# A hybrid recurrent decoder layer: scans behind the first level's multiplications, and a reordered beginning

## Chip, cores and metric

The kernel runs on one core of a Trainium2 chip. The metric is the device time of one execution in microseconds, the median over repeated runs; lower is better.

## The reference

One step of one decoder layer, for a new sequence of 512 tokens and for 8 sequences that go on by one token each (520 columns in all), in float32. A recurrent layer with two branches, then an MLP with squared ReLU; both are scaled and shifted by a modulation that is computed from a conditioning vector. Cut to what is computed:

```python
cs = silu(c)
sh1, sc1, g1, sh2, sc2, g2 = split(cs @ w_mod + b_mod, 6)
h = rmsnorm(x, norm1_g) * (1 + sc1) + sh1
qa, fa, ia, oga, xb, yb, ga, gb = split(h @ w_in, 8)      # 1024 columns each
# branch A: HGRN2, 8 heads: S_t = diag(f_t) S_(t-1) + k_t outer v_t, o_t = S_t^T q_t
o, S_new = hgrn2(silu(qa), k, ia, logf, st_hg)
o_a = rmsnorm(o, hg_onorm_g) * silu(oga)
# branch B: causal conv of width 4, two gates, linear recurrence
xc, buf = causal_conv(xb, st_conv, lru_conv_w, lru_conv_b)
r  = sigmoid(blockdiag(xc, lru_wa) + lru_ba)
ig = sigmoid(blockdiag(xc, lru_wx) + lru_bx)
hseq, h_last = rglru(xc, r, ig, lru_lambda, st_lru)       # h_t = a_t h_(t-1) + sqrt(1 - a_t^2) (i_t x_t)
o_b = hseq * gelu(yb)
merged = sigmoid(ga) * (o_a @ w_branch_a) + sigmoid(gb) * (o_b @ w_branch_b)
x = x + g1 * (merged @ w_out)
h2 = rmsnorm(x, norm2_g) * (1 + sc2) + sh2
x = x + g2 * (square(relu(h2 @ w_ff1)) @ w_ff2)
y = rmsnorm(x, final_norm_g)
```

The outputs are y for both groups of tokens, and the new states of both branches.

## The kernel before

Activations lie transposed: 128 features on the partitions and 520 tokens along a row, 8 such blocks for the width of 1024. Float32 products are made of three reduced-precision ones: weight and activation are each split into a high and a low half, and TensorE (PE) multiplies high by high, high by low and low by high. A tile of weights (1024 x 128) comes by DMA as `wst`; ScalarE (ACT) casts the high half (`whi`, L112), VectorE (DVE) subtracts to get the low one (`wlo`, L115); in the beginning the same two are called `fhi` and `flo`. A product is 128 x 260, half of the 520 columns.

**The order.** Most of the kernel is put in order by the scheduler of the tile framework, from priorities and its own costs; each engine then works its list through, in that order. `behind(ins, first)` (L171) adds an order without a semaphore: `ins` may not be placed ahead of `first`. The beginning, `begin` (from L1575 on), is different: there `self.nc` is a wrapper (`InOrder`, L50) that chains PE, ACT and DVE each in the order in which the code is written.

**The beginning.** Four row blocks of x come in and PE transposes them by a product with the identity into eight PSUM banks, which `whole` copies to SBUF as `xT` (tiles `ma`). Their squares give the norm; `spread_root` spreads the root over the partitions with PE (`pb<-rsd`). `px` is one PSUM tile into which several small transposes go: `rm` (modulation's bias and norms; copied out as `pm`), `xsn` (samples; copied out as `xsr`), and `rb`, `ra`, `rc`, `rd` (parameters of the recurrences, copied out as `pl` and `pa`). The modulation for h comes in four pieces of 256 features: `piece` multiplies the conditioning by 1 MB of `w_mod` (`pt<-wm,cT`) and has ACT copy it out (`modev`), `piece_cols` turns it on PE (`pt<-pick,modev`), `piece_mod` adds and scales on DVE (`modT`). `rooted(k)` multiplies a block of x by the root (`xn<-ma,pb`), `scaled` makes h of it: high half on ACT, low on DVE, and the 8 samples' part on GpSimd (POOL, `fs`). So a piece gives two blocks of h, and `products(n, k, k+1)` adds their 12 products to the n-th of three output tiles (n = 0, 1, 2: the f, q and gate columns of the first head) before the next piece goes on. The three tiles' PSUM slots are `self.first`: two of the pool `mm`, in whose two slots x was transposed (banks 0 and 1 in one, 2 and 3 in the other), and two of `ps`.

**Heads and recurrent branch.** The heads are taken in pairs. `heads_prompt` computes the attention-like matrix within chunks of 128 by levels b = 1, 2, 4, ... 64: at each level PE multiplies pieces of X (L655 for b = 1, L660 for 2 to 32, L664 for 64), then DVE multiplies halves of X by factors in place (L676 for b = 1, L672 after), and PE's next level reads them. PE goes on with the products of the next weight tiles (L151) between two levels. Beside that, `rg_x`, `rg_scans` and `rg_y` work on the recurrent branch in pairs of blocks too: ACT makes exponentials, a square and a root (L825 to L832), DVE multiplies gates (`gate<-gate,xc`, L838), scans (L840), and keeps the last column (L841 to L844); `rg_y` makes the gate y of its output (L853 to L858).

Of the kernel before, what the change touches and what calls it, by code (L numbers as in the profile page):

```python
# [6 lines left out]
F32 = mybir.dt.float32  # L7
# [69 lines left out]
class Kernel:  # L77
# [548 lines left out]
    def heads_prompt(self, hs):  # L626
# [17 lines left out]
        while b < C:  # L644
# [23 lines left out]
            with self.together():  # L668
                for x in range(2):
                    half = halves(x, b, n)  # L670
                    if b > 1:
                        last = nc.vector.tensor_tensor(half, half, factors(tbs, x, b), OP.mult)  # L672
                    else:
                        for e, f in enumerate(fs):
                            t2 = f[:, :L].rearrange("p (n two) -> p n two", two=2)
                            nc.vector.tensor_tensor(half[:, e, :, 0], half[:, e, :, 0], t2[:, :, x], OP.mult)  # L676
            if b == 2:
                self.head_sample_state(hs[1], last)
            if b == 1:
# [138 lines left out]
    def rg_scans(self, ns):  # L818

        nc = self.nc  # L820
        aa = []
        for n in ns:
            r = self.rg[n][0]
            a = self.slot(self.rgp, "ag")
            self.grouped(nc.scalar.activation(a, r, AF.Exp, scale=self.c8n[:, n:n + 1]))  # L825
            self.grouped(nc.scalar.activation(r, r, AF.Tanh, scale=self.c8[:, n:n + 1]))
            u = self.slot(self.rgp, "xc")
            last = nc.scalar.activation(u, a, AF.Square)
            nc.vector.scalar_tensor_tensor(u, u, 1.0, r, OP.add, OP.mult)
            aa.append((a, u))  # L830
        for n, (a, u) in zip(ns, aa):
            root = nc.scalar.activation(u, u, AF.Sqrt)  # L832
            self.behind(root, last)
            last = root
        self.group, self.sigmoids = last, []
        for n, (a, u) in zip(ns, aa):
            g = self.rg[n][1]
            nc.vector.tensor_tensor(g, g, u, OP.mult)  # L838
            hs = self.slot(self.rgp, "hs")
            nc.vector.tensor_tensor_scan(hs[:, :L], a[:, :L], g[:, :L], 0.0, OP.mult, OP.add)  # L840
            nc.vector.tensor_tensor(hs[:, L:], a[:, L:], self.h0[:, :, n], OP.mult)  # L841
            nc.vector.tensor_tensor(hs[:, L:], hs[:, L:], g[:, L:], OP.add)
            nc.vector.tensor_copy(self.hlast[:, n, 0:1], hs[:, L - 1:L])
            nc.vector.tensor_copy(self.hlast[:, n, 1:9], hs[:, L:])  # L844
            self.rg[n] = hs
# [780 lines left out]
    def begin(self):  # L1626
# [74 lines left out]
        self.norm_root()  # L1701
        eye = self.diagonals()
        whole(act, 5, 4, 6, 7)
        whole(dve, 0)
        split_first(0)
        px, pr = ps(), ps()
        own = px[:, 144:457]
        nc.tensor.transpose(px[:, 64:128], rm, self.ident[:64, :64])
        for k in range(KO):
            nc.tensor.transpose(px[:, k * NB:(k + 1) * NB], self.xsn[:, k * 128:(k + 1) * 128], self.ident[:NB, :NB])  # L1710
        spread = pb()
        self.spread_root(spread, pr, *eye)
        pm = self.consts.tile([128, 64], F32, name="pm")
        dve(pm, px[:, 64:128])
# [1 line left out]
        for part in (1, 4):  # L1716
            c = self.bmod[:, part * 8:part * 8 + 8]
            nc.vector.tensor_scalar(c, c, 1.0, None, OP.add)
        whole(act, 1)
        p = self.piece(0, pieces[0])  # L1720
        split_first(1)
        self.piece_cols(p)
        self.xr = self.xn.rearrange("p t d -> p (t d)").rearrange("p (k n) -> p k n", n=L)
        rooted = lambda k: nc.vector.tensor_tensor(self.xr[:, k], self.xT[k][:, :L], spread, OP.mult)

# [7 lines left out]
        rooted(0)  # L1733
        dve(xsr, px[:, :KO * NB].rearrange("p (k b) -> p k b", b=NB))
        nc.vector.tensor_tensor(xs, xsr, pr[:, None, :NB].to_broadcast([128, KO, NB]), OP.mult)
        rooted(1)
        self.piece_mod(p)
        split_rest(0)
        scaled(0, 1)
        split_first(2)  # L1740
        split_rest(1)
        whole(act, 2, 3)
        split_rest(2)

        self.first = [mm()[:, :, :HALF], mm()[:, :, :HALF], [ps()[:, :HALF], ps()[:, :HALF]]]
        acc = [[self.first[0][:, s] for s in range(2)], [self.first[1][:, s] for s in range(2)], self.first[2]]

        def products(n, *ks, only=slice(0, 3)):
# [7 lines left out]

        for i in range(3):
            ks = 2 * i, 2 * i + 1
            products(0, *ks)
            p = self.piece(i + 1, pieces[i + 1])  # L1760
            products(1, *ks, only=slice(0, 1))
            if i == 0:
                nc.tensor.transpose(px[:, 128:144], rb, self.ident[:16, :16])
                self.parameters_in(own, *par)
                pl = self.hc.tile([128, 16], F32, name="pl")
                dve(pl, px[:, 128:144])
                dve(self.pa, self.pa_ps)
            self.piece_cols(p)
            rooted(2 * i + 2)
            self.piece_mod(p)  # L1770
            rooted(2 * i + 3)
            scaled(2 * i + 2, 2 * i + 3)
            products(1, *ks, only=slice(1, 3))
            if i == 1:
                self.bounds(pl)
                self.exponentials()
                nc.scalar.activation(self.act0, self.act0, AF.Sigmoid)
            products(2, *ks)
        for k in range(KO):
            pool.tensor_copy(self.xT[k][:, L:], xsr[:, k])  # L1780
            pool.dma_start(self.xT_d[k], self.xT[k])
# [124 lines left out]
```

## Time and profile before

| | us |
|---|---|
| median of 3 runs | 1017.22 |
| lowest, highest | 1016.69, 1019.72 |
| the profiled execution | 1015.0 |
| its span in the trace | 1013.2 |
| PE busy | 992.3 (98%) |
| DVE busy | 673.8 (67%) |
| ACT busy | 512.2 (51%) |
| POOL busy | 130.4 (13%) |

The profiled execution is one of its own; times of single instructions come from it. A row of the timeline gives start, duration (us), engine, line, operation, written tile <- read tiles, shapes and count, and in brackets the idle time of the engine before it with what ended it. Neighbouring instructions of a kind stand in one row, whose duration goes from the first one's start to the last one's end. A row's start counts from the start of the span. The beginning takes until 53 us; the two stretches with the long waits of PE among the heads lie at 288 and 378 us.

### The profile page before, as it was taken

The page shows a single profiled execution, that of the slowest core. Times are in us where ns is not written, and L with a number is a line of the kernel's source. Part 1 is how long each engine was busy: PE and PEld are TensorE (multiplying, and loading weights), DVE is VectorE, ACT ScalarE, POOL GpSimd, SP SyncE. Part 2 cuts the span into 40 slices and gives each one's busy share as a digit, 9 for nine tenths or more (in the row PEclk, how much of TensorE's full clock was granted, in tenths as well). Part 3 has the DMA queues.
Part 4 walks back from the last instruction along what each step waited for, and adds up shares of the span by engine and source line. Part 5 has one row for each costly group of instructions (what it writes and reads, how often), then busy time and mean ns, then how long its engine had stood idle before and what let it go on. Part 6 is the DMA issues. An engine that isn't in the chain of part 4 may idle for free. (4 is left out here: it accounts for less than half of the span.)

```text
span 1013.2 us, 23554 instructions
## 1 busy us (share of the span) xinstructions
PE 992.3 (98%) x9738; PEld 964.7 (95%) x9738; DVE 673.8 (67%) x1417; ACT 512.2 (51%) x963; POOL 130.4 (13%) x253
## 2 busy tenths in 40 slices
PE   6999999999999999999999999999999999999997
PEld 5899999999989999999999999999999999999996
DVE  7686867695785867346233448777767776777685
ACT  6364745735654573345111224466555645646663
POOL 4320000000000010002000000022321331232050
PEclk9999999999999999999999999999999999999998
DMA  9974354344344444339756787322672483273242
GB/s 298 314 214 119 97 164 127 103 122 135 107 137 116 124 147 127 95 98 304 205 167 177 231 245 207 102 86 50 151 176 64 98 196 104 53 175 86 63 84 85
DMA packets 205373, 145.80 MB, mean 144 GB/s; under 512 B 6742, under 2 KB 193774, under 8 KB 205258
## 3 DMA queue, kind: packets, MB, share of 16 engines
q1 hardware_dynamic: 194034, 128.08, 43.1%
q0 software_dynamic: 11216, 16.18, 7.4%
q8 instruction: 76, 1.25, 0.5%
q14 instruction: 31, 0.25, 0.1%
q10 hardware_dynamic: 16, 0.03, 0.0%
HBM read 123.61 MB, written 13.39 MB: 135 GB/s over the span
## 5 line engine op out<-in xcount | busy, mean ns | idle before, releaser
L151 PE MATMUL mm<-h,whi 128*128 128x260 f32 (+1 forms) x2944 | 488.5, 285 | 0.0
L151 PEld LDWEIGHTS mm<-h,whi 128*128 128x128 f32 x2944 | 409.2, 188 | 2.9 <-issue 1.4
L151 PE MATMUL mm<-h,wlo 128*128 128x260 f32 x1472 | 302.4, 285 | 0.0
L115 DVE TENSOR_TENSOR wlo<-wst,whi 128x1024 fp32r<-128x1024 f32 x164 | 200.0, 1221 | 133.5 <-ACT whi L112 132.2
L112 ACT CAST whi<-wst 128x1024 fp32r<-128x1024 f32 x164 | 171.7, 1049 | 213.6 <-PE mm L151 166.2
L151 PEld LDWEIGHTS mm<-h,wlo 128*128 128x128 f32 x1472 | 229.5, 188 | 0.9 <-issue 0.6
L151 PE MATMUL mm<-a,whi 128*128 128x260 f32 x512 | 83.0, 284 | 0.0
L151 PEld LDWEIGHTS mm<-a,whi 128*128 128x128 f32 x512 | 70.0, 188 | 2.1 <-ACT whi L112 1.6
L885 POOL DMA_DIRECT2D t<-obT_d x8 | 4.3, 541 | 396.9 <-PE pb L790 300.1
L151 PE MATMUL mm<-a,wlo 128*128 128x260 f32 x256 | 51.4, 282 | 0.0
L1262 DVE TENSOR_TENSOR f<-f 128x260 f32<-128x260 f32 x64 | 27.3, 426 | 27.8 <-ACT f L1257 27.2
L1254 POOL TENSOR_TENSOR ft<-ft,fsh 128x8 f32<-128x8 f32 x28 | 18.4, 658 | 206.6 <-DVE ft L1248 206.6
L1251 ACT ACTIVATE ft<-ft,fsh 128x512 f32<-128x512 f32 (+2 forms) x36 | 24.0, 675 | 36.0 <-DVE ft L1248 36.0
L151 PE MATMUL mm<-b,whi 128*128 128x260 f32 x256 | 41.7, 285 | 0.0
L151 PEld LDWEIGHTS mm<-a,wlo 128*128 128x128 f32 x256 | 39.4, 188 | 0.0
L151 PEld LDWEIGHTS mm<-b,whi 128*128 128x128 f32 x256 | 35.0, 188 | 2.1 <-ACT whi L112 2.1
L672 DVE TENSOR_TENSOR X<-X,tb 128x512 f32<-128x512 f32 x48 | 30.9, 684 | 5.4 <-PE ps L660 4.2
L1296 POOL DMA_DIRECT2D ma<-snap x28 | 26.5, 960 | 40.1 <-issue 32.3
L1278 POOL DMA_DIRECT2D ma<-snap x28 | 26.4, 943 | 38.0 <-DMA ma<-snap 22.7
L1257 ACT ACTIVATE f<-ft 128x520 f32<-128x520 f32 (+1 forms) x36 | 20.8, 587 | 15.0 <-POOL ft L1255 13.0
L580 ACT ACTIVATE st<-st,fkq 128x128 f32<-128x128 f32 x64 | 19.8, 395 | 14.1 <-DMA st<-in_state_hgrn_dram 12.4
L151 PE MATMUL mm<-b,wlo 128*128 128x260 f32 x128 | 25.6, 282 | 0.0
(576 smaller groups left out, 1865.5 us busy)
## 6 DMA issues: line engine op xcount, KB each, us to landing
wst<-in_w_in_dram SPq DMA_DIRECT2D x64, 512.0 KB, 4.1
wst<-in_w_mod_dram SPq DMA_DIRECT2D x32, 512.0 KB, 3.8
wst<-in_w_ff_dram SPq DMA_DIRECT2D x64, 256.0 KB, 3.6
wst<-in_w_ff_dram SPq DMA_DIRECT2D x32, 512.0 KB, 4.7
wm<-in_w_mod_dram SPq DMA_DIRECT2D x8, 1024.0 KB, 10.8
st<-in_state_hgrn_dram SPq DMA_DIRECT2D x8, 512.0 KB, 6.7
vb<-vd SPq DMA_DIRECT2D x8, 512.0 KB, 3.7
out_dram<-st SPq DMA_DIRECT2D x8, 512.0 KB, 3.9
```

The costliest lines, as they stand in the source:

```text
L112: ins = self.nc.scalar.copy(hi, st)
L115: self.nc.vector.tensor_tensor(lo, st, hi.bitcast(F32), OP.subtract)
L151: self.last_product = self.nc.tensor.matmul(ps[s][:, :c.stop - c.start], x, y[:, c], start=first and n == 0, stop=last and n == 2)
L580: nc.scalar.activation(st[:, b], st[:, b], AF.Copy, scale=fkq[:, 0, b:b + 1])
L672: last = nc.vector.tensor_tensor(half, half, factors(tbs, x, b), OP.mult)
L885: nc.gpsimd.dma_start(t, self.obT_d[n])
L1251: nc.scalar.activation(t[:, :p], t[:, :p], AF.Relu, bias=sh[:, 0:1])
L1254: eng.tensor_tensor(t[:, p:], t[:, p:], sh[:, 1:9], OP.add)
L1257: nc.scalar.activation(f, self.two(self.ft)[:, a:a + n], AF.Square)
L1262: self.nc.vector.tensor_tensor(f[:, n], f[:, a], f[:, b], op)
L1278: nc.gpsimd.dma_start(x[1][:, b], v[:, :n], accum_op=OP.add)
L1296: nc.gpsimd.dma_start(x[t][:, a], s[p], accum_op=OP.add)
```

## The change

In `rg_scans` the two gate multiplications of a pair are kept in `self.scans`; in `heads_prompt` they are put behind the last of the level-1 multiplications of X. Each scan reads its gate, so it follows. In `begin`, nineteen transposes of the identity into PSUM tiles that are overwritten later are added at four places (9, 3, 4 and 3), the copies of banks 0 and 1 go to ACT behind the first cast, the first low half `flo` moves ahead of the first scaling, the casts for tiles 1 and 2 move behind the first h, the parameters' transposes move ahead of the first products and their copies from DVE to ACT, and in the first round tiles 0 and 1 get their products ahead of the second piece.

```diff
@@ -673,7 +673,10 @@
                     else:
                         for e, f in enumerate(fs):
                             t2 = f[:, :L].rearrange("p (n two) -> p n two", two=2)
-                            nc.vector.tensor_tensor(half[:, e, :, 0], half[:, e, :, 0], t2[:, :, x], OP.mult)
+                            last = nc.vector.tensor_tensor(half[:, e, :, 0], half[:, e, :, 0], t2[:, :, x], OP.mult)
+            if b == 1:
+                for ins in self.scans:
+                    self.behind(ins, last)
             if b == 2:
                 self.head_sample_state(hs[1], last)
             if b == 1:
@@ -828,6 +831,7 @@
             last = nc.scalar.activation(u, a, AF.Square)
             nc.vector.scalar_tensor_tensor(u, u, 1.0, r, OP.add, OP.mult)
             aa.append((a, u))
+        self.scans = []
         for n, (a, u) in zip(ns, aa):
             root = nc.scalar.activation(u, u, AF.Sqrt)
             self.behind(root, last)
@@ -835,7 +839,7 @@
         self.group, self.sigmoids = last, []
         for n, (a, u) in zip(ns, aa):
             g = self.rg[n][1]
-            nc.vector.tensor_tensor(g, g, u, OP.mult)
+            self.scans.append(nc.vector.tensor_tensor(g, g, u, OP.mult))
             hs = self.slot(self.rgp, "hs")
             nc.vector.tensor_tensor_scan(hs[:, :L], a[:, :L], g[:, :L], 0.0, OP.mult, OP.add)
             nc.vector.tensor_tensor(hs[:, L:], a[:, L:], self.h0[:, :, n], OP.mult)
@@ -1701,14 +1705,22 @@
         self.norm_root()
         eye = self.diagonals()
         whole(act, 5, 4, 6, 7)
-        whole(dve, 0)
         split_first(0)
+        whole(act, 0, 1)
+
+        def busy(out, n):
+
+            for _ in range(n):
+                nc.tensor.transpose(out[:, :128], self.ident, self.ident)
+
+        spread = pb()
+        busy(spread, 9)
         px, pr = ps(), ps()
         own = px[:, 144:457]
         nc.tensor.transpose(px[:, 64:128], rm, self.ident[:64, :64])
         for k in range(KO):
             nc.tensor.transpose(px[:, k * NB:(k + 1) * NB], self.xsn[:, k * 128:(k + 1) * 128], self.ident[:NB, :NB])
-        spread = pb()
+        busy(spread, 3)
         self.spread_root(spread, pr, *eye)
         pm = self.consts.tile([128, 64], F32, name="pm")
         dve(pm, px[:, 64:128])
@@ -1716,10 +1728,14 @@
         for part in (1, 4):
             c = self.bmod[:, part * 8:part * 8 + 8]
             nc.vector.tensor_scalar(c, c, 1.0, None, OP.add)
-        whole(act, 1)
+        split_rest(0)
         p = self.piece(0, pieces[0])
-        split_first(1)
+        self.first = [mm()[:, :, :HALF]]
+        busy(self.first[0][:, 0], 4)
         self.piece_cols(p)
+        nc.tensor.transpose(px[:, 128:144], rb, self.ident[:16, :16])
+        self.parameters_in(own, *par)
+        busy(self.first[0][:, 0], 3)
         self.xr = self.xn.rearrange("p t d -> p (t d)").rearrange("p (k n) -> p k n", n=L)
         rooted = lambda k: nc.vector.tensor_tensor(self.xr[:, k], self.xT[k][:, :L], spread, OP.mult)
 
@@ -1733,16 +1749,19 @@
         rooted(0)
         dve(xsr, px[:, :KO * NB].rearrange("p (k b) -> p k b", b=NB))
         nc.vector.tensor_tensor(xs, xsr, pr[:, None, :NB].to_broadcast([128, KO, NB]), OP.mult)
+        self.piece_mod(p)
         rooted(1)
-        self.piece_mod(p)
-        split_rest(0)
         scaled(0, 1)
+        split_first(1)
         split_first(2)
+        pl = self.hc.tile([128, 16], F32, name="pl")
+        act(pl, px[:, 128:144])
+        act(self.pa, self.pa_ps)
         split_rest(1)
         whole(act, 2, 3)
         split_rest(2)
 
-        self.first = [mm()[:, :, :HALF], mm()[:, :, :HALF], [ps()[:, :HALF], ps()[:, :HALF]]]
+        self.first += [mm()[:, :, :HALF], [ps()[:, :HALF], ps()[:, :HALF]]]
         acc = [[self.first[0][:, s] for s in range(2)], [self.first[1][:, s] for s in range(2)], self.first[2]]
 
         def products(n, *ks, only=slice(0, 3)):
@@ -1756,26 +1775,23 @@
 
         for i in range(3):
             ks = 2 * i, 2 * i + 1
-            products(0, *ks)
+            n = 1 if i else 2
+            for m in range(n):
+                products(m, *ks)
             p = self.piece(i + 1, pieces[i + 1])
-            products(1, *ks, only=slice(0, 1))
-            if i == 0:
-                nc.tensor.transpose(px[:, 128:144], rb, self.ident[:16, :16])
-                self.parameters_in(own, *par)
-                pl = self.hc.tile([128, 16], F32, name="pl")
-                dve(pl, px[:, 128:144])
-                dve(self.pa, self.pa_ps)
+            products(n, *ks, only=slice(0, 1))
             self.piece_cols(p)
             rooted(2 * i + 2)
             self.piece_mod(p)
             rooted(2 * i + 3)
             scaled(2 * i + 2, 2 * i + 3)
-            products(1, *ks, only=slice(1, 3))
+            products(n, *ks, only=slice(1, 3))
             if i == 1:
                 self.bounds(pl)
                 self.exponentials()
                 nc.scalar.activation(self.act0, self.act0, AF.Sigmoid)
-            products(2, *ks)
+            if i:
+                products(2, *ks)
         for k in range(KO):
             pool.tensor_copy(self.xT[k][:, L:], xsr[:, k])
             pool.dma_start(self.xT_d[k], self.xT[k])
```

How this moves instructions, at three places. On PE, at the beginning, from the first piece (`pt<-wm,cT`) to the second; before:

```order
L69 MATMUL pt<-wm,cT 32x256 x8
L69 MATMUL pt<-pick,modev 128x9 x2
L69 MATMUL mm<-h,fhi 128x260 x8
L69 MATMUL mm<-h,flo 128x260 x4
L69 MATMUL pt<-wm,cT 32x256 x8
L69 MATMUL mm<-h,fhi 128x260 x4
L69 MATMUL ps<-ident,ra 128x16
L69 MATMUL ps<-ident,rb 128x57
L69 MATMUL ps<-ident,rc 128x64
L69 MATMUL ps<-ident,rd 128x96 x2
L69 MATMUL pt<-pick,modev 128x9 x2
```

and now (`mm<-ident` are identity transposes):

```order
L69 MATMUL pt<-wm,cT 32x256 x8
L69 MATMUL mm<-ident 128x128 x4
L69 MATMUL pt<-pick,modev 128x9 x2
L69 MATMUL ps<-ident,ra 128x16
L69 MATMUL ps<-ident,rb 128x57
L69 MATMUL ps<-ident,rc 128x64
L69 MATMUL ps<-ident,rd 128x96 x2
L69 MATMUL mm<-ident 128x128 x3
L69 MATMUL mm<-h,fhi 128x260 x8
L69 MATMUL mm<-h,flo 128x260 x4
L69 MATMUL mm<-h,fhi 128x260 x8
L69 MATMUL mm<-h,flo 128x260 x4
L69 MATMUL pt<-wm,cT 32x256 x8
```

The transposes of `ra` to `rd` come ahead of the first product, and 24 products of tiles 0 and 1 (12 before) ahead of the second piece.

On ACT, from the first cast to the second `modev`; before:

```order
L69 CAST fhi<-wst 128x1024
L69 COPY ma<-mm 128x512
L69 COPY modev<-pt 128x256
L69 CAST fhi<-wst 128x1024
L69 ACTIVATE h<-xn,modT 128x512 x2
L69 CAST fhi<-wst 128x1024
L69 COPY ma<-mm 128x512 x2
L69 COPY modev<-pt 128x256
```

and now:

```order
L69 COPY ma<-mm 128x512 x2
L69 COPY modev<-pt 128x256
L69 ACTIVATE h<-xn,modT 128x512 x2
L69 CAST fhi<-wst 128x1024 x2
L69 COPY pl<-ps 128x16
L69 COPY pa<-ps 128x313
L69 COPY ma<-mm 128x512 x2
L69 COPY modev<-pt 128x256
```

The two `ma<-mm` copies of banks 2 and 3 now stand behind h, two casts and the two copies that were DVE's. On DVE at the same place the rows from the first scaling on were

```order
L69 TENSOR_TENSOR xn<-ma,pb 128x512
L69 COPY xsr<-ps 128x64
L69 TENSOR_TENSOR xhs<-xsr,ps 128x64
L69 TENSOR_TENSOR xn<-ma,pb 128x512
L69 TENSOR_TENSOR modT<-pt,pm 128x18
L69 TENSOR_TENSOR modT<-modT,pm 128x18
L69 TENSOR_TENSOR flo<-wst,fhi 128x1024
L69 SCALAR_TENSOR_TENSOR h<-xn,modT,h 128x512 x2
L69 TENSOR_TENSOR flo<-wst,fhi 128x1024 x2
L69 COPY pl<-ps 128x16
```

and are, from the copy of pm on:

```order
L69 COPY pm<-ps 128x64
L69 TENSOR_SCALAR pm<-pm 128x8 x2
L69 TENSOR_TENSOR flo<-wst,fhi 128x1024
L69 TENSOR_TENSOR xn<-ma,pb 128x512
L69 COPY xsr<-ps 128x64
L69 TENSOR_TENSOR xhs<-xsr,ps 128x64
L69 TENSOR_TENSOR modT<-pt,pm 128x18
L69 TENSOR_TENSOR modT<-modT,pm 128x18
L69 TENSOR_TENSOR xn<-ma,pb 128x512
L69 SCALAR_TENSOR_TENSOR h<-xn,modT,h 128x512 x2
L69 TENSOR_TENSOR flo<-wst,fhi 128x1024 x2
```

The low half `flo` is ahead of the first `xn`, and `modT` is behind one scaling in place of two.

On DVE, in the third pair of heads, from the second gate on; before:

```order
L838 TENSOR_TENSOR gate<-gate,xc 128x520
L840 SCALAR_TENSOR_TENSOR hs<-ag,gate 128x512
L842 TENSOR_TENSOR hs<-hs,gate 128x8
L841 TENSOR_TENSOR hs<-ag,pa 128x8
L840 SCALAR_TENSOR_TENSOR hs<-ag,gate 128x512
L843 COPY hlast<-hs 128x1
L115 TENSOR_TENSOR wlo<-wst,whi 128x1024
L844 COPY hlast<-hs 128x8
L842 TENSOR_TENSOR hs<-hs,gate 128x8
L843 COPY hlast<-hs 128x1
L676 TENSOR_TENSOR X_798<-X_798,ma 128x256 x2
L855 SCALAR_TENSOR_TENSOR y<-y 128x520
```

and now:

```order
L115 TENSOR_TENSOR wlo<-wst,whi 128x1024
L676 TENSOR_TENSOR X_817<-X_817,ma 128x256 x2
L859 SCALAR_TENSOR_TENSOR y<-y 128x520
L676 TENSOR_TENSOR X_817<-X_817,ma 128x256 x2
L842 TENSOR_TENSOR gate<-gate,xc 128x520 x2
L684 TENSOR_TENSOR a_4018<-ps,mdiag 128x256
L861 TENSOR_TENSOR y<-y 128x520
L844 SCALAR_TENSOR_TENSOR hs<-ag,gate 128x512
L846 TENSOR_TENSOR hs<-hs,gate 128x8
L845 TENSOR_TENSOR hs<-ag,pa 128x8
L844 SCALAR_TENSOR_TENSOR hs<-ag,gate 128x512
L688 COPY_PREDICATED a_4018<-mask_179,ps 128x256
```

Both gates and both scans went from ahead of the four `X<-X,ma` to behind them; `wlo` stayed ahead. In the first two pairs the order was this way round before, and doesn't change; in the fourth pair the four multiplications stand together, and nothing of the recurrent branch but the small `hs<-ag,pa` right ahead of them. Between the levels b = 2 and b = 4 of the third pair PE now has 46 products (31 before), and between b = 4 and b = 8 of the fourth 51 (38 before).

## The prediction

> **What bounds the kernel now.** I read the page's busy times first, then the waits of PE, then the stretches around those waits.
>
> ```profile
> span 1013.2 us, 23554 instructions
> PE 992.3 (98%) x9738; PEld 964.7 (95%) x9738; DVE 673.8 (67%) x1417; ACT 512.2 (51%) x963; POOL 130.4 (13%) x253
> ```
>
> PE is busy for 992.3 of 1013.2 us, so all that any edit here can win is the 21 us in which it stands still, and time in which it runs at a lower clock. The waits of PE (what it waited for: us in total, times, longest) tell which of these the change reaches:
>
> ```profile
> PE ps L660 <- DVE X L676: 3.3, 4, 1.0
> PE mm L69 <- ACT h L69: 2.5, 1, 2.5
> ```
>
> The first row is the level-2 products of the heads, waiting for the level-1 multiplications; the second is the first product of the beginning, waiting for h. The other waits (for inputs at the very start, one or two tenths elsewhere) are left as they are.
>
> The beginning, as PE and the clock saw it:
>
> ```profile
> 16.80 0.61 PE L69 MATMUL pt<-pick,modev 128*128 128x9 f32 x4 [0.49 <-ACT modev L69]
> 19.91 2.28 PE L69 MATMUL mm<-h,fhi 128*128 128x260 f32 x8 [2.50 <-ACT h L69]
> 23.10 1.30 PE L69 MATMUL pt<-wm,cT 128*32 128x256 f32 x16
> 25.01 0.23 PE L69 MATMUL ps<-ident,ra 16*128 16x16 f32 x1
> 25.44 0.38 PE L69 MATMUL ps<-ident,rd 96*128 96x96 f32 x2
> 27.09 1.12 PE L69 MATMUL ps<-h,fhi 128*128 128x260 f32 x8
> 28.04 0.64 PE L69 MATMUL ps<-h,flo 128*128 128x260 f32 x4
> 30.50 1.07 PE L69 MATMUL pt<-wm,cT 128*32 128x256 f32 x16
> ```
>
> At full clock eight products take 28.04 - 27.09 = 0.95 us, 0.12 each. The first twelve took from 19.91 to 23.10, about 3.2 us, and the windows (length, PE busy, granted clock, DMA share, GB/s) say why:
>
> ```profile
> 16.80:20.20 3.40, 0.90 (x6) 1.00 1.14 323
> 20.20:23.60 3.40, 3.31 (x20) 0.50 1.09 348
> ```
>
> After a stretch with 0.90 us busy of 3.40 the clock was halved for the next 3.40 us. So the old beginning pays twice: 2.50 us idle, and then up to 1.7 us (half of 3.4) of slow clock.
>
> **The beginning, part by part.** Seven things move. I follow each engine, because most of the new order is a matter of what is queued behind what.
>
> ```profile
> 17.52 0.18 DVE L69 TENSOR_TENSOR modT<-pt,pm 128x18 f32<-128x18 f32 x1 [0.37 <-PE pt L69]
> 17.82 1.22 DVE L69 TENSOR_TENSOR flo<-wst,fhi 128x1024 fp32r<-128x1024 f32 x1
> 19.89 1.41 DVE L69 SCALAR_TENSOR_TENSOR h<-xn,modT,h 128x512 fp32r<-128x512 f32 x2 [0.85 <-ACT h L69]
> 25.95 0.48 DVE L69 COPY pa<-ps 128x313 f32<-128x313 f32 x1
> 19.14 1.33 ACT L69 ACTIVATE h<-xn,modT 128x512 fp32r<-128x512 f32 x2
> 20.38 1.03 ACT L69 CAST fhi<-wst 128x1024 fp32r<-128x1024 f32 x1
> 21.32 1.05 ACT L69 COPY ma<-mm 128x512 f32<-128x512 f32 x2
> 17.99 1.12 POOL L69 TENSOR_TENSOR fs<-xhs,modT 128x16 f32<-128x16 f32 x1 [6.42 <-DVE modT L69]
> ```
>
> The 19 identity transposes are put where PE waits anyway. Windows of the first transposes give their price:
>
> ```profile
> 7.00:9.90 2.90, 2.90 (x16) 1.00 1.04 363
> 9.90:11.40 1.50, 1.50 (x13) 1.00 1.15 311
> ```
>
> Thirteen in 1.50 us is 0.115 each (the earlier 16 ran at 0.18). Nine take 1.0 us after 11.40, three 0.35, four 0.5 between the piece and the pick, three 0.35 after the transposes of ra to rd: all covered, by the wait for ACT's and DVE's first results, by modev, and by the wait for h. Uncovered, the last seven would cost 0.8 us.
>
> The transposes of ra, rb, rc and rd go ahead of the first products. They take 25.44 + 0.38 - 25.01 = 0.8 us, and stand behind the pick (from 16.80, its four passes about 0.4), so they end near 18.0. They write the same PSUM tile px from which DVE copies xsr, and that copy stands ahead of modT on DVE. So modT, ready to start at 17.52 before, now waits for rd: 18.0, plus xsr and xhs (about 0.4), first modT at 18.45, second done by 18.85. That is a new wait, 0.9 us on modT. It costs little on h, because ACT's h formerly stood behind a cast (fhi of tile 1), and started at 19.14; now that cast is behind it and h starts at 18.87. First product: 19.91 - 0.27 = 19.64. POOL's sample part starts 0.9 later too and its 1.12 us, with a cast behind, ends near 20.4: the second half of the first product waits for that, while h's low parts are later anyway.
>
> The split's low half flo (1.22 us of DVE) moves ahead of the first scaling, into time in which DVE waited. DVE's low halves of h follow ACT's by about 0.75, and end near 20.9 (19.89 + 1.41 = 21.3 before). Of the twelve products of tile 0 the last six need the last low half: 20.9 + 6 x 0.12 = 21.6 to 21.7, against 23.06 before. So far 1.4 us won, if the clock holds: between 16.80 and 20.20 PE is now busy for about 0.4 + 0.8 + 0.35 + 0.55 = 2.1 us in place of 0.90.
>
> Now tile 1's products are ahead of the second piece, and they write the PSUM slot that still holds the transposed x of banks 2 and 3. ACT empties it, behind everything it got: h until 20.2, two casts of 0.97 each (their step, 21.32 - 20.38 is 0.94) until 22.15, pl and pa, which are now ACT's (0.2 + 0.45), until 22.75, the two copies (1.05) until 23.6 to 23.7. Before, they ended at 22.4 and nobody waited. So PE idles from 21.7 to 23.65, **a new wait of about 1.95 us**. If the copies came first it would be gone.
>
> Tile 1's twelve products end at 23.65 + 1.42 = 25.07, and the second piece starts there: 1.97 us later than its 23.10. The chain from a piece to h is seen at the next piece, which started at 30.50:
>
> ```profile
> 31.69 0.37 ACT L69 COPY modev<-pt 128x256 f32<-128x256 f32 x1 [3.00 <-PE pt L69]
> 32.83 0.18 DVE L69 TENSOR_TENSOR modT<-pt,pm 128x18 f32<-128x18 f32 x1 [2.71 <-PE pt L69]
> 33.26 1.34 ACT L69 ACTIVATE h<-xn,modT 128x512 fp32r<-128x512 f32 x2 [1.20 <-DVE modT L69]
> 34.02 1.42 DVE L69 SCALAR_TENSOR_TENSOR h<-xn,modT,h 128x512 fp32r<-128x512 f32 x2 [0.20 <-ACT h L69]
> ```
>
> From piece to last low half 34.02 + 1.42 - 30.50 = 4.94 us. So the second pair of h is whole at 25.07 + 4.94 = 30.0, and six more products of tile 0 bring the third piece to 30.7, against 30.50. What is saved in products after the piece (12 of them, tile 1's, which stood behind it before) turns into idle time on PE, since the chain is what ends last. **The beginning: +0.2 us**, the order behind it is unchanged and PE full, so that the shift stays. Bounds: if the slot were free in time, the piece would start near 23.1 with tile 1 done, and the third piece be paced 1.8 us earlier (-1.8); if the clock closes as well, +1.7 on top (below).
>
> **The scans.** Only where the scans stood ahead of the level-1 multiplications can the new order move anything. In the first two pairs of heads they stood behind them before; the order changes in the third and fourth pair, the two places with the long waits.
>
> ```profile
> 283.20 0.70 DVE L838 TENSOR_TENSOR gate<-gate,xc 128x520 f32<-128x520 f32 x1 [1.06 <-ACT xc L832]
> 284.51 1.21 DVE L840 TENSOR_TENSOR_SCAN hs<-ag,gate 128x512 f32<-128x512 f32 x1
> 286.97 1.21 DVE L115 TENSOR_TENSOR wlo<-wst,whi 128x1024 fp32r<-128x1024 f32 x1
> 288.31 0.75 DVE L676 TENSOR_TENSOR X<-X,ma 128x256 f32<-128x256 f32 x2
> 288.98 0.68 DVE L855 SCALAR_TENSOR_TENSOR y<-y 128x520 f32<-128x520 f32 x1
> 292.22 1.28 DVE L672 TENSOR_TENSOR X<-X,tb 128x512 f32<-128x512 f32 x2
> 293.43 2.17 DVE L602 SCALAR_TENSOR_TENSOR st<-vb,fkq,st 128x128 f32<-128x128 f32 x8
> 284.07 1.05 ACT L112 CAST whi<-wst 128x1024 fp32r<-128x1024 f32 x1
> 289.21 0.46 PE L660 MATMUL ps<-X 128*32 128x32 f32 x32 [0.92 <-DVE X L676]
> 290.39 0.46 PE L660 MATMUL ps<-X 128*32 128x32 f32 x32 [0.73 <-DVE X L676]
> ```
>
> and the windows over this place and the same one of the fourth pair:
>
> ```profile
> 288.00:291.00 3.00, 1.35 (x68) 1.00 0.44 129
> 378.00:381.00 3.00, 1.31 (x68) 1.00 0.97 342
> ```
>
> Here PE loses 0.92 + 0.73 = 1.65 us, and in the fourth pair as much (3.0 - 1.31 = 1.69).
>
> Third pair: gates and scans (2 x 0.70 + 2 x 1.21 = 3.8 us) leave the front, but wlo stays there, and wlo needs ACT's whi, done at 284.07 + 1.05 = 285.1. So wlo ends at 286.3, X's first half at 287.0, y at 287.7, X's second at 288.35. PE now reaches level 2 after 21 products in place of 29, 8 x 0.12 = 0.96 earlier (287.2). The first half waits for nothing, the second until 288.35, about 0.8 us after 287.55. Gain 0.8. Then the 3.8 us stand ahead of the level-2 multiplications: gates, mask work, y, scans and the first X add up to about 5.9 us, and PE has 46 products (5.5 us, 31 before) plus its own level to cover it: short by 0.2. Net 0.6.
>
> Fourth pair: X stands right behind level 1, with neither wlo nor scans ahead: four multiplications 1.5 us against 16 products and four transposes, 2.3 us. The 1.69 us go. Then DVE has, between level 4 and level 8, gates, state updates (2.17), y, scans and X, some 7.5 us ahead of X's first half, against 51 products (6.1 us) and the level's own 0.7: short by up to 0.7, and a gate that waits for ACT's root holds all that. Net 1.69 less 1.0 = 0.7, or less.
>
> Together 1.3 us at best reckoning; as I counted only the first paybacks and the later levels (four more in each pair) stand behind the moved scans as well, I take 0.9. Bounds: 3.3 if nothing is paid back, and a loss of 2 if two levels per pair each miss their cover by 1 us and a half of the gain is lost.
>
> **Sum.** +0.2 - 0.9 = -0.7 us on the profiled execution of 1015.0 us (span 1013.2, 1.8 us around it), so 1014.3; the median of the runs shown is 1017.22, 2.2 above that execution, so **1016.5 us**.
>
> **The rivals.**
>
> *The clock closes in the new gap (slower).* Place: 20.20 to 23.60, now busy only from 20.2 to 21.7, 1.5 us of 3.4 (44%); and again 27.0 to 30.4, where products of two tiles are done and the next wait for h, about as much. For it: with 0.90 of 3.40 it closed. Against it: 288 to 291 was busy 1.35 of 3.0 (45%) and stayed at 1.00. One closure halves the clock for 3.4 us and costs up to 1.7, as PE's products then pace the piece: 1016.5 + 1.7 = 1018.2, both 1019.9. [...]
>
> *The slot is free in time and the stalls vanish (faster).* The gap needs ACT to run as reckoned; if PE's wait were not on those copies, the beginning wins 1.8; with both stalls gone for good, 3.3. Together 1017.2 - 5.1 = 1012.1; one of them, 1014. Against: ACT's queue is in order, 3.5 us of work stand between h and the slot.
>
> *The scans displace later levels (slower).* As bounded: +2 in place of -0.9, 1017.2 + 0.2 + 2 = 1019.4. For it: 3.8 us of DVE work go from a place with one wait to one with six levels behind it. Against: PE's own order leaves 46 and 51 products where 31 stood, and later X rows had slack.
>
> *The identity transposes don't hold the clock.* Then 20.2 to 23.6 is at half clock as before, tile 0 ends near 22.4, still ahead of 23.65: no change to the sum.
>
> **How the numbers follow.** Forecast 0.48 (with the last rival's 0.05 in it), clock 0.27, faster 0.14, displaced scans 0.11. What this kernel's measurement tells from no change is about 0.3%, 3.05 us: under 1014.17 or above 1020.27. Faster: most of the faster case, 0.13. Slower: both closures, or scans and clock together, 0.10. Same 0.77. The forecast's own range is 1015.3 to 1017.5; the clock rival takes it to 1019.4, half of the faster case down to 1014.0.
>
> **What would show it.** Right: first product near 19.6, PE idle near 21.7 to 23.6 put down to ACT's ma copy; second piece near 25, third near 30.7; no wait for L676 in the fourth pair, about 0.8 in the third, new waits for the later X rows. Wrong: a second piece before 24; a granted clock of 0.50 between 23.6 and 27 or 30.4 and 34; waits for L672 above 1.5 us together.

## The result, and the profile after

| | before | changed |
|---|---|---|
| median, 12 runs each (us) | 1017.86 | 1018.03 |
| lowest to highest (us) | 1015.46 to 1019.72 | 1016.06 to 1019.67 |
| ratio to before, 95% interval | | 1.0001 (0.9990 to 1.0012) |
| profiled execution, its span (us) | 1015.0, 1013.2 | 1019.46, 1017.7 |

No change that can be measured, as forecast. The two profiles are 4.5 us apart all the same, each within its kernel's spread, so a difference between them must be shown to come of the change before it is put down to it. PE's waits in the changed kernel, as far as they differ from before (what it waited for: us in total, times, longest):

```profile
PE ps L588 <- ACT ma L565: 1.6, 1, 1.6
PE mm L69 <- ACT h L69: 1.6, 2, 1.3
PE mm L151 <- DVE wlo L115: 1.1, 1, 1.1
PE pt L725 <- ACT g L721: 0.8, 2, 0.5
PE mm L69 <- ACT ma L69: 0.7, 1, 0.7
PE ps L660 <- DVE X L676: 0.7, 1, 0.7
```

The 3.3 us for L676 are down to 0.7 and the 2.5 us for h to 1.6 in two waits; four are new or longer: for the PSUM slot (ACT ma L69), for wlo, for g, and one near 149 us, in a stretch whose order the change leaves alone. The beginning on PE and DVE:

```profile
18.24 0.49 PE L69 MATMUL mm<-ident 128*128 128x128 f32 x3
20.03 2.25 PE L69 MATMUL mm<-h,fhi 128*128 128x260 f32 x8 [1.29 <-ACT h L69]
22.08 1.07 PE L69 MATMUL mm<-h,flo 128*128 128x260 f32 x4
23.88 2.10 PE L69 MATMUL mm<-h,fhi 128*128 128x260 f32 x8 [0.73 <-ACT ma L69]
26.78 1.80 PE L69 MATMUL pt<-wm,cT 128*32 128x256 f32 x16
33.37 1.07 PE L69 MATMUL pt<-wm,cT 128*32 128x256 f32 x16
...
18.44 0.22 DVE L69 COPY xsr<-ps 128x64 f32<-128x64 f32 x1 [1.21 <-PE ps L69]
18.84 0.17 DVE L69 TENSOR_TENSOR modT<-pt,pm 128x18 f32<-128x18 f32 x1
```

The waits that the prediction named in the beginning are there: xsr 1.21 us behind the transposes of `ra` to `rd`, modT at 18.84, the first product waiting for h, tile 1 waiting for ACT's copies. The third piece comes at 33.37 in place of 30.50. The windows (length, PE busy, granted clock, DMA share, GB/s) show what most of that is:

```profile
17.80:21.20 3.40, 2.00 (x14) 1.00 1.11 339
21.20:24.60 3.40, 2.57 (x11) 0.54 1.09 351
24.60:28.00 3.40, 3.40 (x23) 0.50 1.11 337
```

The clock was halved for two stretches of 3.4 us, from about 21.4 to 28.3 (granted clock 0.50), where before had one. In the third pair of heads:

```profile
289.06 1.05 ACT L112 CAST whi<-wst 128x1024 fp32r<-128x1024 f32 x1
290.14 1.22 DVE L115 TENSOR_TENSOR wlo<-wst,whi 128x1024 fp32r<-128x1024 f32 x1 [2.92 <-ACT whi L112]
291.28 0.76 DVE L676 TENSOR_TENSOR X<-X,ma 128x256 f32<-128x256 f32 x2
293.37 0.46 PE L660 MATMUL ps<-X 128*32 128x32 f32 x32 [0.67 <-DVE X L676]
302.64 1.21 DVE L115 TENSOR_TENSOR wlo<-wst,whi 128x1024 fp32r<-128x1024 f32 x1
303.91 0.50 PE L151 MATMUL mm<-h,wlo 128*128 128x260 f32 x2 [1.12 <-DVE wlo L115]
```

X waits for wlo, and wlo 2.92 us for whi, so of 1.65 us of PE's wait 0.67 stay. Ten microseconds later the next wlo, whose whi had been cast from 295.38 on, is reached by DVE only at 302.64, behind gates, scans and state updates, and PE waits 1.12 us for it.

### The profile page after: what moved, and what is told of

Read it like the earlier page. It is cut to its first block, busy times and chain, and to the rows that moved or that the text cites. A ratio compares the mean times of both kernels' runs of the same rounds, so it can differ in the third digit from the quotient of the medians.

```text
span 1017.7 us, 23582 instructions
## 1 busy us (share of the span) xinstructions
PE 998.0 (98%) x9757; PEld 968.3 (95%) x9757; DVE 673.1 (66%) x1414; ACT 512.9 (50%) x966; POOL 129.3 (13%) x253
## 5 line engine op out<-in xcount | busy, mean ns | idle before, releaser
L1266 DVE TENSOR_TENSOR f<-f 128x260 f32<-128x260 f32 x64 | 27.3, 427 | 27.8 <-ACT f L1261 27.2
L672 DVE TENSOR_TENSOR X<-X,tb 128x512 f32<-128x512 f32 x48 | 30.8, 683 | 4.0 <-PE ps L664 3.0
L1282 POOL DMA_DIRECT2D ma<-snap x28 | 26.3, 940 | 43.7 <-DMA ma<-snap 28.3
L580 ACT ACTIVATE st<-st,fkq 128x128 f32<-128x128 f32 x64 | 19.8, 396 | 18.0 <-DMA st<-in_state_hgrn_dram 14.3
```

The source lines that it names most:

```text
L580: nc.scalar.activation(st[:, b], st[:, b], AF.Copy, scale=fkq[:, 0, b:b + 1])
L1266: self.nc.vector.tensor_tensor(f[:, n], f[:, a], f[:, b], op)
L1282: nc.gpsimd.dma_start(x[1][:, b], v[:, :n], accum_op=OP.add)
```

## The experiments

Each kernel ran beside runs of the kernel before on the same chip. The clock is the mean over a kernel's runs of TensorE's granted clock (before: 0.991 to 0.992 beside each group). e5 had 6 runs and e7 had 7, the others 10 or 12. The groups (e1 to e4, e5 to e8, e9 to e11, e12) did not all run on one chip, so a kernel is compared first with the before beside it.

| edit | median us | before beside it | ratio, 95% interval | clock |
|---|---|---|---|---|
| e1 scans only | 1016.90 | 1017.93 | 0.9986 (0.9966 to 1.0006) | 0.992 |
| e2 beginning only | 1019.21 | 1017.93 | 0.9999 (0.9976 to 1.0023) | 0.994 |
| e3 copies first | 1016.09 | 1017.93 | 0.9974 (0.9953 to 0.9995) | 0.995 |
| e4 xsr first | 1015.34 | 1017.93 | 0.9972 (0.9955 to 0.9989) | 0.997 |
| e5 both of these | 1014.42 | 1018.60 | 0.9950 (0.9933 to 0.9968) | 0.997 |
| e6 no identity transposes | 1017.73 | 1018.60 | 0.9990 (0.9974 to 1.0007) | 0.992 |
| e7 both, no identity transposes | 1014.75 | 1018.60 | 0.9956 (0.9938 to 0.9975) | 0.993 |
| e8 both, scans as before | 1016.86 | 1018.60 | 0.9982 (0.9969 to 0.9995) | 0.995 |
| e9 scans only, again | 1015.75 | 1017.98 | 0.9980 (0.9963 to 0.9998) | 0.994 |
| e10 beginning only, again | 1018.74 | 1017.98 | 1.0004 (0.9989 to 1.0019) | 0.994 |
| e11 the change, again | 1017.23 | 1017.98 | 0.9990 (0.9975 to 1.0004) | 0.995 |
| e12 before with identity transposes | 1017.89 | 1018.38 | 0.9993 (0.9972 to 1.0013) | 0.994 |

**e1 and e9, the scans alone** (the three hunks in `heads_prompt` and `rg_scans`, on the kernel before).

> The kernel before with the scans' order alone. Theory (the scans' gain is paid back by later waits of the same pairs): PE's waits for L676 fall from 3.3 us to about 0.7, and new waits of PE among the heads (for wlo, for X at later levels, for g) come to 1.5 to 2.7 us; the time is 0.2 to 1 us under that of before. Rival (the two halves of the change each move the time by 2 us or more and cancel): new waits under 1 us, the time 2 us or more under that of before.

> The scans' order alone once more, on one chip with the next two, for the size of each half. Theory (the scans win about 1 us, the beginning loses about 1 by the clock, and the change is their sum): 0.5 to 2 us under before. Rival (both halves are nothing, and the differences of the first runs were noise): within 0.5 us of before.

PE's waits for L676 fell to 0.7, that for wlo (1.1) came, and the medians are 1.0 and 2.2 us under before, the second with an interval clear of 1. The theory's mechanism holds. Its size is read better from the traces, between two waits that all profiles have, for e (L622) and for os (L397); in before they are

```profile
193.31 0.65 PE L622 MATMUL pt<-ident,sev 128*128 128x128 f32 x4 [0.65 <-DVE e L751]
452.41 1.50 PE L397 MATMUL pt<-wst,cT 128*32 128x256 f32 x24 [0.27 <-DVE os L624]
```

From the start of the one wait to the start of the other, before took 452.15 - 192.66 = 259.49, e1 453.88 - 195.47 = 258.41, and e9 453.11 - 194.68 = 258.43: 1.1 us less, of the 2.6 less that PE waited for X. The change itself gives 456.59 - 197.27 = 259.32 in its first profile and 454.22 - 195.67 = 258.55 in e11, so 0.2 to 0.9. Over all profiles with a granted clock of 1.00 there, the four kernels without the new order (before, e2, e10, e12) take 259.1 to 259.5, mean 259.3, and the nine profiles with it 258.0 to 259.3, mean 258.5. So the scans' order is worth about 0.8 us; what the medians show beyond that isn't shown to come of it.

These two kernels also begin exactly as before does, and their beginnings are slower than the one in before's profile. The clock was halved from 13.7 to 27.3 in e1 and from 16.2 to 26.4 in e9, against 20.2 to 23.6 in before, and the third piece came late (e1, then e9):

```profile
33.22 1.07 PE L69 MATMUL pt<-wm,cT 128*32 128x256 f32 x16
32.39 1.07 PE L69 MATMUL pt<-wm,cT 128*32 128x256 f32 x16
```

So before's 30.50 is the earliest of three profiles of the old beginning, and a later third piece in one profile of the new beginning is no loss by itself.

**e2 and e10, the beginning alone** (the changed kernel without the hunk that calls `behind`).

```diff
-            if b == 1:
-                for ins in self.scans:
-                    self.behind(ins, last)
```

> The whole change without the order of the scans. Theory (the beginning wins h and loses it again in the wait for the PSUM slot): first product near 19.6 to 20.0, a gap of PE of 0.7 to 2 us ahead of tile 1's products, third piece at 30.7 with full clock and up to 33.4 where the clock closes; the time is within 1 us of before or up to 3 above it. Rival (the beginning wins and the scans lose): third piece under 29.5, the time 1.5 us or more under that of before.

> The beginning alone once more. Theory: 0.5 to 2 us above before, mean clock no higher than before's although the identity transposes run. Rival: within 0.5 us of before.

Medians 1.3 and 0.8 us above before, ratios that can't be told from 1. The mean clock, in e10's theory no higher than before's, was 0.994 in both against 0.992: if the beginning loses anything, it isn't by a lower mean clock. The two profiles differ in the beginning mainly by the clock. e2's was halved from about 20.4 to 27.2, its third piece came at 32.92; e10's stayed at 1.00, third piece at 31.62, though PE stood still for longer in the slot's place:

```profile
20.29 1.95 PE L69 MATMUL mm<-h,fhi 128*128 128x260 f32 x8 [1.30 <-ACT h L69]
24.15 1.22 PE L69 MATMUL mm<-h,fhi 128*128 128x260 f32 x8 [1.43 <-ACT ma L69]
25.78 1.07 PE L69 MATMUL pt<-wm,cT 128*32 128x256 f32 x16
31.62 1.07 PE L69 MATMUL pt<-wm,cT 128*32 128x256 f32 x16
```

At a granted clock of 1.00 the wait for the slot is 1.42 to 1.43 (e4, e10, e11); at a halved one it is 0.70 to 0.73 (the change, e2, e6). Tile 1's products started 3.85 to 3.86 us behind tile 0's in all six.

**e11, the change once more**, for the clock.

> The changed kernel itself beside them. [...] Rival (the closed clock of the first profile was chance): granted clock 1.00 from 17 to 31.

It came out as the rival says: the same kernel whose first profile was halved for 6.8 us shows, over the same stretches,

```profile
17.80:21.20 3.40, 2.10 (x15) 1.00 1.11 335
21.20:24.60 3.40, 1.78 (x12) 1.00 1.09 352
24.60:28.00 3.40, 3.40 (x35) 1.00 1.10 342
```

less work in the middle one, and full clock; it stayed at 1.00 from 17 to 31. So the clock was halved behind these waits in one execution of this kernel and not in the other. Third piece: 32.04, with a first piece 0.92 later than before's (16.15, waiting for nothing of the change); 31.1 when that is taken off, 0.6 above before's 30.50 and under e1's and e9's.

**e3, the copies first.**

```diff
         whole(act, 0, 1)
+        whole(act, 2, 3)
...
         split_rest(1)
-        whole(act, 2, 3)
```

> The whole change, with ACT's copies of banks 2 and 3 right behind those of banks 0 and 1 (ACT stands idle there). Theory (tile 1's products wait for these copies alone): no gap between tile 0's products and tile 1's, the second piece 0.7 to 1.9 us earlier than in the changed kernel at the same clock, third piece near 29 at full clock. Rival (another wait, for the cast or the low half of tile 1, takes the place): a gap of PE of over 0.4 us in the same place, with another releaser.

The gap is gone, with no other in its place:

```profile
19.63 2.28 PE L69 MATMUL mm<-h,fhi 128*128 128x260 f32 x8 [1.29 <-ACT h L69]
21.71 1.07 PE L69 MATMUL mm<-h,flo 128*128 128x260 f32 x4
22.57 1.37 PE L69 MATMUL mm<-h,fhi 128*128 128x260 f32 x8
24.34 1.07 PE L69 MATMUL pt<-wm,cT 128*32 128x256 f32 x16
30.19 1.07 PE L69 MATMUL pt<-wm,cT 128*32 128x256 f32 x16
```

Tile 1 waited for these copies alone. The wait for h is as in the change, and the clock was halved behind it, from about 19.7 to 23.1; so the third piece, expected near 29 at full clock, came at 30.19. With the gap gone the clock was halved for one stretch of 3.4 us; with it, in the change's first profile and in e2, for two, in e10 and e11 not at all.

**e4, xsr first**: the first scaling and the copy of xsr are written ahead of the transposes of `rb` and of `parameters_in`.

```diff
         self.piece_cols(p)
...
+        rooted(0)
+        dve(xsr, px[:, :KO * NB].rearrange("p (k b) -> p k b", b=NB))
         nc.tensor.transpose(px[:, 128:144], rb, self.ident[:16, :16])
...
-        rooted(0)
-        dve(xsr, px[:, :KO * NB].rearrange("p (k b) -> p k b", b=NB))
```

> The whole change, with the first scaling and DVE's copy of xsr written ahead of the transposes of ra to rd, so that the copy doesn't wait for them. Theory (modT is late because xsr waits for the transposes): modT starts at 17.6 to 17.9 in place of 18.84, h, POOL's part and the slot's copies all about 1 us earlier, second and third piece 1 us earlier at the same clock. Rival (something else holds modT): modT stays at 18.6 or later.

```profile
16.91 0.22 DVE L69 COPY xsr<-ps 128x64 f32<-128x64 f32 x1
17.55 0.18 DVE L69 TENSOR_TENSOR modT<-pt,pm 128x18 f32<-128x18 f32 x1
...
18.75 1.96 PE L69 MATMUL mm<-h,fhi 128*128 128x260 f32 x8 [0.23 <-ACT h L69]
22.61 1.22 PE L69 MATMUL mm<-h,fhi 128*128 128x260 f32 x8 [1.42 <-ACT ma L69]
30.07 1.07 PE L69 MATMUL pt<-wm,cT 128*32 128x256 f32 x16
```

modT 1.3 us earlier, and the wait for h 0.23 in place of 1.29. The clock rose to 0.997 over ten runs (the changed kernel: 0.995), with the slot's wait still there.

**e5, both edits.**

> The whole change with both edits: banks 2 and 3 copied early, and xsr copied ahead of the transposes of ra to rd. Theory (the two waits that the change made, for the slot and behind the transposes, are all that the beginning loses, and each is removed by its own edit): neither the 1.3 us wait for h nor the 0.7 to 1.4 us wait for the slot, third piece at 28.4 to 28.9, mean clock 0.996 or more, time 3 to 5 us under the changed kernel and 2.5 to 5 under before. Rival (the third piece is set by something else, the weights or POOL): third piece at 29.8 or later, time that of the single edits.

```profile
19.86 1.96 PE L69 MATMUL mm<-h,fhi 128*128 128x260 f32 x8 [0.24 <-ACT h L69]
22.14 1.13 PE L69 MATMUL mm<-h,fhi 128*128 128x260 f32 x8
23.68 1.07 PE L69 MATMUL pt<-wm,cT 128*32 128x256 f32 x16
29.52 1.07 PE L69 MATMUL pt<-wm,cT 128*32 128x256 f32 x16
```

The wait for the slot is gone and that for h is 0.24, at 1014.42 us, 4.2 under before, ratio 0.9950 (0.9933 to 0.9968): a small gain, but clear of the noise, and faster than both kernels. The third piece at 29.52 misses the expected 28.4 to 28.9; x came later in this execution (first piece at 16.38, 1.15 later than before's), and in e8, which begins in the same way, the piece came at 28.79. From the start of the last transpose of x to the third piece it is 17.94 us, against 19.36 in before, 19.31 in e3, 19.36 in e4 (1.0 less than in e11, as its theory has it at the same clock), 21.62 and 20.39 in the two profiles of the change, and 21.9 and 21.1 in e1 and e9 with before's beginning.

**e6 and e7, without the identity transposes** (the four calls of `busy` taken out of the changed kernel and of e5).

> The whole change without the nineteen identity transposes. Theory (the clock closes in the changed kernel although they run, since PE idles from 18.7 to 20.0 behind them; they add nothing else): time and mean clock as the changed kernel's, within 1 us and 0.002. Rival (they keep the clock open for the first products): mean clock lower by 0.002 or more, time 1 to 2 us longer.

> Both edits, without the nineteen identity transposes. Where the wait for h is gone, the transposes fill the rest of the way up to the first product. Theory (they matter only where no longer gap follows): mean clock 0.002 or more under that of both edits with them, 0.5 to 2 us longer. Rival (they count for nothing): same clock, same time.

In both the mean clock falls, 0.995 to 0.992 and 0.997 to 0.993: in this they hold what the rivals, or the theory of e7, said, and the profiles are halved from about 14.5 on. The time doesn't follow: 1017.73 against 1018.03, and 1014.75 against 1014.42, neither told apart. A possible reason stands in the profiles: the wait for ACT's ma (L565), 1.6 us in the change and 1.3 in e5, isn't there in e6 and e7. That this makes up for the clock isn't shown.

**e8, both edits without the scans' order.**

> Both edits of the beginning, without the order of the scans. Theory (the scans win about 0.7 to 1 us, paid back otherwise): waits for L676 back at 3.3 us, no wait for wlo, time 0.3 to 1.5 us over that with the scans' order. Rival (the scans' order is worth 2 us or more, or nothing): 2 us over, or none.

2.4 us over e5, which is what the rival said (2 us or more) and more than the theory's 0.3 to 1.5; the two intervals barely miss each other. The waits are as expected (L676 3.3, none for wlo); but here the clock was halved behind the fourth pair's wait (PE busy for 1.20 of 2.50 us from 378.5 to 381), which it was not in before's profile (1.27 of 2.50, granted clock 1.00):

```profile
377.00:381.00 4.00, 2.31 (x75) 0.95 0.96 331
381.00:384.40 3.40, 3.40 (x18) 0.55 0.42 143
```

The stretch between the waits for e and os took 453.73 - 192.53 = 261.20 here, 1.9 more than in the kernels of the same order at full clock. So in this execution more was lost there than the waits' own length; how often that happens isn't known, and so neither is how much of the 2.4 us it makes.

**e12, before with the identity transposes.**

> The kernel before with the nineteen identity transposes alone, at the same places beside its own order (9 and 3 ahead of the root's spreading, 4 and 3 around the first pick). Two questions. First, PE's wait of 1.2 to 1.8 us for ACT's ma (L565) near 147 us, behind a state's load that lands late: it stands in seven of eight profiles of kernels with the transposes and in none of five without. Theory (the transposes bring it): it comes here. Rival (it comes of the new beginning's times, or by chance): it doesn't. Second, the clock: before waits 2.5 us for h, of which three transposes fill 0.4. Theory (what closes the clock is the wait for h): granted clock halved somewhere between 17 and 31 us and mean clock within 0.002 of before's 0.992, time within 1 us of before. Rival (the transposes alone hold the clock): mean clock 0.996 or more, time 1.5 us or more under before.

The wait for L565 doesn't come: the transposes alone don't bring it. It stands in seven of eight profiles of kernels that have both the new beginning and the transposes (1.2 to 1.8 us; not in e3), and in none of the six others. ACT waits there for a head's state (L580) that lands late (before, then the change):

```profile
142.82 0.69 ACT L580 ACTIVATE st<-st,fkq 128x128 f32<-128x128 f32 x2 [4.10 <-DMA st<-in_state_hgrn_dram]
147.44 0.69 ACT L580 ACTIVATE st<-st,fkq 128x128 f32<-128x128 f32 x2 [5.85 <-DMA st<-in_state_hgrn_dram]
```

The seven have 5.5 to 6.1 us of this wait, the others 4.1 to 4.3. Why it lands late stays open. Time (0.5 under before) and mean clock (0.994) are as the second theory has them. The clock was halved once more behind the wait for h:

```profile
16.80:20.20 3.40, 1.15 (x9) 1.00 1.14 326
20.20:23.60 3.40, 2.93 (x16) 0.54 1.08 349
```

## Why the prediction was right, and where its steps were not

The forecast, no measurable change, with a small gain (-0.7), came out as +0.2 (-1.0 to +1.2); 1018.0 lies in the range. It lies above the forecast's own part of it (up to 1017.5), but the before measured with it was 0.6 above the median from which the forecast was reckoned.

The two halves have the signs that the prediction gave them. In the medians the scans alone win 1.0 and 2.2 us (forecast 0.9) and the beginning alone loses 0.8 and 1.3 (forecast 0.2), but only one of these four can be told from no change. The traces say where the time is. Up to PE's product of L588, its wait taken off, the old beginning takes 145.87, 148.65 and 147.85 us (before, e1, e9) and the new one 148.88, 147.57, 148.42 and 147.16 (change, e11, e2, e10): 0.5 us more in the mean, far less than the old one's own spread. Then comes the wait for L565, 1.2 to 1.8 us, which no term of the sum held. The scans give back 0.8. The rest is alike in all fourteen profiles: 46.8 us from L588 to the wait for e, and 560.8 to 561.9 from the wait for os to the end. So the scans' term was about right, and the beginning's 0.2 left out a wait of about 1.5 us. These parts add up to about 1.2 us slower, the upper end of the measured interval; they are single executions.

Some luck is in the agreement. The sum starts from one profile of before, 2.2 us under the median, in whose beginning the clock was halved for 3.4 us, and adds these 2.2 us unchanged. Other profiles of the same beginning were halved for 13.6 and 10.2 us (e1, e9). The new one's halved clock (6.8 us in two of its four profiles) may not show in the time because the old one's was halved even longer in two of its three.

- *First product near 19.6, h 0.27 earlier than before.* The step holds, the size is 0.4 off: 20.03, since xsr, named as a new wait, was passed at 18.44 where 18.0 had been reckoned; x itself was 0.3 later too. A wait for h of 1.3 us is left in every profile that has this order with its identity transposes, about what the reckoned 2.1 us busy of 3.40 leaves. What was put at too little is this wait: behind it the clock was halved in the change's first profile, e2 and e3 (not in e10 and e11), and e4 shows that the transposes ahead of xsr make most of it (0.23 in place of 1.29).
- *The slot's wait.* Right in place and cause (e3), 0.7 with a halved clock and 1.4 with a full one, for a reckoned 1.95.
- *The third piece 0.2 later at full clock.* Two profiles at full clock give about 0.6 later than before's profile, and earlier than the other two of before's beginning. Second and third piece at 26.78 and 33.37 in the first profile, for about 25 and 30.7, are mostly the halved clock's: e11 and e10, at full clock, have them at 26.19 and 25.78, 32.04 and 31.62.
- *The clock as a rival with 0.27.* The granted clock of 0.50 between 23.6 and 27, named as a sign against the forecast, is in the first profile and not in e11. The clock did get halved, and the place is half right: in the first profile this began behind the wait for h, near 21.4, and went on for two stretches of 3.4 us with the slot's gap, for one without it in e3; that the gap prolonged it isn't shown, as e10 and e11 have both waits at 1.00. With the wait for h gone and the gap left (e4) the mean clock was 0.997. And it was no either-or: the same kernel was halved for 6.8 us in one profile and not in another, so the rival belongs to the kernel's own spread, as in before's beginning (3.4, 13.6 and 10.2 us). No run shows a busy share above which the clock stays at 1.00: behind 2.00 us of 3.40 it was halved in the first profile, behind 1.78 of 3.40 it was not in e11.
- *"288 to 291 was busy 45% and stayed at 1.00", as evidence against it.* That step fails: in e8 the clock was halved behind the same kind of stall, busy for 1.20 of 2.50 us (48%).
- *The third pair: wlo stays ahead, wait about 0.8.* 0.67. *The fourth: none.* 0.17 us for L672 is all that is left there.
- *Paybacks at later X levels.* About right in amount, wrong in place. X's later levels cost 0.4 us in all (0.2 before); the payback is wlo, 1.12 us, as DVE's moved scans stand ahead of it, in all nine profiles with the new order. The 0.8 us for g in the first profile are 0.2 to 0.3 in e1, e9 and e11 and not shown to be the scans'.
- *"The order behind it is unchanged and PE full, so that the shift stays."* Wrong by the wait for L565, 1.6 us near 149, which neither the order nor the waits of before showed; its cause is open. It is larger than the rest of what the beginning adds in the traces, 0.5.

## What to carry to other kernels

Where an engine's work is moved ahead to fill a wait, look at which tile it writes: four small transposes into a shared PSUM tile held back a copy, and with it h; writing that copy ahead of them took the wait for h from 1.3 to 0.23 us. Before a product is moved ahead, ask what still holds its PSUM slot, and where in its engine's queue that stands; here ACT stood idle for 1.48 us ahead of modev, and with the copies put earlier (e3) the gap was gone. And a chain of small waits can't be judged from one profile: here the clock was halved for 6.8 us in one execution of a kernel and not at all in another. Take several profiles of the kernel before too, and compare a stretch between two events that all of them have, at the same granted clock: the 0.8 us of the scans show there, and hardly in medians of runs that spread over several us.

## What the runs showed of the hardware

The clock was halved in one execution of a kernel and not in another. In the change's two profiles the stretch 17.8 to 21.2 was busy 2.00 and 2.10 us of 3.40, and the clock was halved for 6.8 us after the one and not at all after the other; before's beginning was halved for 3.4, 13.6 and 10.2 us in three profiles (before, e1, e9). The halvings in the beginnings lasted 3.4 us in before, e3 and e12, 6.8 in the change and e2, 10.2 in e9, 13.6 in e1, 13.7 in e7 and 17.2 in e6; e4, e5, e8, e10 and e11 had none there.

With the identity transposes the mean granted clock was higher in all three pairs of kernels that differ in them alone (0.995 and 0.992, not on one chip; 0.997 and 0.993; 0.994 and, for the 17 runs of before beside e12, 0.991).
